# First chunk of a hybrid decoder layer: two column tiles of its projection worked on half of its tokens at a time

## The chip, the core and the metric

The kernel runs on one core of one Trainium2 chip. The metric is the device time in microseconds of one execution. The engines are PE (TensorE: matmuls and transposes), DVE (VectorE), ACT (ScalarE), POOL (GpSimd) and SP (SyncE, which here only issues DMAs). Each engine works through its own queue in order, and waits on semaphores of the others.

## The reference

One layer, 2048 tokens of width 1024. A root-mean-square norm, one projection to 4096 columns that are split in six parts, two token mixers (a state-space branch on `ua`, a pooling branch on `ub`) with gates, an output projection, a residual and a second norm. All in float32.

```python
def _rmsnorm(x, g):
    x32 = x.astype(jnp.float32)
    y = x32 * lax.rsqrt(jnp.mean(x32 * x32, axis=-1, keepdims=True) + EPS)
    return y.astype(x.dtype) * g

h = _rmsnorm(x, norm_g[l])
proj = h @ w_in[l] + b_in[l]
ua, za, ub, zb, ga, gb = jnp.split(proj, SPLITS, axis=-1)
...
merged = (jax.nn.sigmoid(ga) * (ya @ w_branch_a[l])
          + jax.nn.sigmoid(gb) * (yb @ w_branch_b[l]))
x = x + merged @ w_out[l]
return _rmsnorm(x, final_norm_g)
```

## The kernel before

The tokens are worked in four chunks `c` of 512, the columns of the projection in tiles `n` of 128. A chunk is four x tiles of 128 tokens by 1024. Each is normed (sum of squares, reciprocal root, scaling), and turned by PE transposes into `hT[c]`, which has the 1024 channels as eight blocks `k` of 128 partitions, and 512 tokens as columns.

Float32 precision comes from splitting every operand in a high and a low part, both in the format fp32r: `split` (line 94) has ACT write the high part (L96), and then another engine subtract it from the source for the low part (L98 with plain sources on DVE or POOL, L100 with a scale, on DVE). `mm3` (line 103) then issues three matmuls, L104 high by high, L105 high by low part of hT, L106 low part of the weights by high. So L105 needs DVE's low part of hT, and L106 the low part of the weight tile.

`rsqrt` (line 108) has nine tiny DVE instructions, L113 to L122, behind one for the mean (L545). Weight tiles pass through `pump` (line 133): it splits the next loaded weight tile and issues a further load (`load_next`, L163, on SP's queue, two raw buffers). For the input projection the low part of the weights is made on POOL.

`first_block` (line 565) is the special start: four x tiles of chunk 0 are squared on ACT (`mean_square`, L543), one root for all four, then each tile is scaled in two halves of its channels, two tiles on ACT (L574), two on DVE (L576). `transpose_tile` (line 559, L562) turns one block `k` of all four tiles into one PSUM tile of 512 columns and splits it. Blocks are turned two ahead of the eight steps of the first column tile. The second column tile of chunk 0, and all later ones, are `proj_block` (line 593): 24 matmuls with 512 columns in a row. PSUM tiles for transposes (`mstile`) have four buffers, and so have those for the projection (`mmtile`).

The order of the program's work is the order in which the code calls the engines; nothing reorders it. In the loop at line 628 the first chunk's column tile 0 is followed by `pump` (third weight tile, `w_first`), the bias and store of the tile (L637, L638), the norm of chunk 1 (`norm_tiles`), then column tile 1, `pump` for the fourth weight tile, tile 2, four transposed blocks of chunk 1, tile 3 and four more blocks. Loads are issued by SP in this order: four x tiles of chunk 0, weight tiles 0 and 1 (W0, W1 below; W2 and W3 are the third and fourth), four x tiles of chunk 1, W2, chunk 2. Before all this, `WARM` transposes of the identity run on PE (L623).

Of the kernel before, what the change touches and what calls it, by code (L numbers as in the profile page):

```python
# [9 lines left out]
F32 = mybir.dt.float32  # L10
# [3 lines left out]
ALU = mybir.AluOpType  # L14
# [15 lines left out]
WINDOWS = (2, 4, 8, 16)  # L30
EPS = 1e-6
MAGIC = 12582912.0
WARM = 17


@with_exitstack
def hybrid_kernel(ctx: ExitStack, tc: tile.TileContext, x, norm_g, w_in, b_in, log_dt, lam_re, lam_im,
# [31 lines left out]
    def mmtile(name="mm"):  # L69
        return pmm.tile([128, 512], F32, tag="mm", name=name)  # L70

    def mstile(name="ms"):
        return pms.tile([128, 512], F32, tag="ms", name=name)
# [20 lines left out]
    def split(src, hi, lo, scale=None, eng=None):  # L94

        A.activation(hi, src, AF.Copy, scale=1.0 if scale is None else scale)  # L96
        if scale is None:
            (eng or V).tensor_tensor(out=lo, in0=src, in1=hi.bitcast(F32), op=ALU.subtract)  # L98
        else:
            V.scalar_tensor_tensor(out=lo, in0=src, scalar=scale, in1=hi.bitcast(F32),  # L100
                                   op0=ALU.mult, op1=ALU.subtract)
# [28 lines left out]
    def add_job(key, load, target):  # L130
        jobs.append((key, load, target))

    def pump():

        j = state["split"]
        while state["loaded"] < min(j + 2, len(jobs)):
            load_next()
        key, raw, target = jobs[j][0], jobs[j][3], jobs[j][2]
        hi, lo, view = target(key)
        split(view(raw), hi, lo, scale={"ya": 0.125, "yb": 0.5}.get(key[0]), eng=GP if key[0] in ("in", "out", "glu") else V)  # L140
        state["split"] = j + 1
        if state["loaded"] < len(jobs):
            load_next()

# [372 lines left out]

    xts = {}

    def load_x(c):  # L520

        for i in range(4):
            tt = 4 * c + i
            if c in (1, 2):
                xt = xp.tile([128, D], F32, tag="xt", bufs=8, name="xt")
            else:
                xt = d1.tile([128, D], F32, tag="xt", bufs=4, name="xt")
            k0 = (tt % 2) * 128
            SP.dma_start(out=xt, in_=xr[tt // 2, k0:k0 + 128, :])
            xts[tt] = xt  # L530
# [28 lines left out]
    def transpose_tile(c, k):  # L559
        ps = mstile("psT")  # L560
        for i in range(4):
            PE.transpose(ps[:, i * 128:(i + 1) * 128], xts[4 * c + i][:, k * 128:(k + 1) * 128], idn)  # L562
        split(ps, hT[c][:, 0, k, :], hT[c][:, 1, k, :], scale=gcol(k))

    def first_block():

        rstd = mean_square(0)
        pump()

        def scale(h):  # L570
            for i in range(4):
                xt = xts[i][:, h * 512:(h + 1) * 512]
                if i % 2:
                    A.activation(xt, xt, AF.Copy, scale=rstd[:, i:i + 1])  # L574
                else:
                    V.tensor_scalar(out=xt, in0=xt, scalar1=rstd[:, i:i + 1], scalar2=None, op0=ALU.mult)  # L576

        load_x(2)
        scale(0)
        transpose_tile(0, 0)  # L580
        transpose_tile(0, 1)
        scale(1)
        ps = mmtile()
        w = hl[("in", UA)].rearrange("p s (k n) -> p s k n", k=NK)
        for k in range(NK):
            if k + 2 < NK:
                transpose_tile(0, k + 2)
            if k == 3:
                pump()
            mm3(ps, w[:, 0, k, :], w[:, 1, k, :], hT[0][:, 0, k, :], hT[0][:, 1, k, :], k == 0, k == NK - 1)  # L590
        return ps

    def proj_block(n, c):
        ps = mmtile()
# [5 lines left out]
    warm = d1.tile([128, 1], F32, name="warm")  # L600
    GP.memset(warm, 0.0)
    A.activation(warm, warm, AF.Tanh)
    load_x(0)
    rows = d1.tile([48, 128], F32, name="rows")
    A.dma_start(out=rows[0:32, :], in_=b_in[0].rearrange("(n p) -> n p", p=128))
    A.dma_start(out=rows[32:40, :], in_=norm_g[0].rearrange("(n p) -> n p", p=128))
# [14 lines left out]
    psw = mstile("psw")  # L621
    for i in range(WARM):
        PE.transpose(psw[:, (i % 4) * 128:(i % 4 + 1) * 128], idn, idn)  # L623
    load_next()
    load_next()
    load_x(1)
    pv = Later(V)
    for c in range(NCH):
        for n in range(NB):
            ps = proj_block(UA + n, c) if c or n else first_block()  # L630
            if c == 0 and n < 2:
                pump()
            if c == 0 and n == 0:
                small = load_params(par)
                load_x(3)
            o = stg.tile([128, 512], F32, tag="stg", name="uo")
            A.activation(o, ps, AF.Identity, bias=bcol(UA + n))  # L637
            A.dma_start(out=Ud[n][2 * c:2 * c + 2].rearrange("j g c k -> (g c) j k"),  # L638
                         in_=o.rearrange("p (j k) -> p j k", j=2))
            if c + 1 < NCH:  # L640
                if n == 0 and c == 0:
                    norm_tiles(1)
                if n >= 2:
                    for k in range(4 * n - 8, 4 * n - 4):
                        transpose_tile(c + 1, k)
                    if (c, n) == (1, 3):
                        s_x.close()
                        open_hT(3)
                if n == 3 and c + 2 < NCH:
                    norm_tiles(c + 2)  # L650
            if c == NCH - 1 and n < 2:
                pump()
            if (c, n) == (1, 0):
                params(par, pv, *small)
            pv.issue(18)
# [570 lines left out]
```

## Time and profile before

| | |
|---|---|
| median of 3 runs | 1210.48 us (1209.46 to 1212.61) |
| profiled execution | 1210.43 us |
| its span | 1208.6 us |
| PE busy | 1177.1 us, 97% |
| DVE busy | 735.7 us, 61% |
| ACT busy | 395.4 us, 33% |
| POOL busy | 345.6 us, 29% |

The span is the time from the first to the last recorded instruction; the execution has 1.8 us more around it. Busy time of PE overlaps itself, since a matmul starts before the one ahead has ended: for PE the spacing of starts says how long a piece of work takes. A row of the timeline that has "x4" stands for four instructions in a row, and its length is that of all. What stands in brackets is how long the engine was idle, and what ended that.

### The profile page before, as it was taken

The numbers are of one execution on the slowest core, as the hardware profiler recorded it, in microseconds if no ns is written. First come the engines' busy times: TensorE is split into PE (matmuls) and PEld (weight loads), VectorE is DVE, ScalarE is ACT, GpSimd is POOL, SyncE is SP. The second block draws the span as 40 slices with busy tenths as digits, with TensorE's granted clock in tenths as the row PEclk, the third lists the DMA queues.
The fourth block names the chain that finished last, engine by engine and source line by source line (L and its number), as shares of the span: only waits on it lengthen the run. The fifth ranks groups of instructions, "written<-read, shape, count | busy, mean of one in ns | idle before, by whom it ended". The sixth has DMA issues, their size and how long they took to land. (4 is left out here: it accounts for less than half of the span.)

```text
span 1208.6 us, 14777 instructions
## 1 busy us (share of the span) xinstructions
PE 1177.1 (97%) x5413; PEld 974.5 (81%) x5413; DVE 735.7 (61%) x1310; ACT 395.4 (33%) x622; POOL 345.6 (29%) x232
## 2 busy tenths in 40 slices
PE   6999999999999999999999999999999999999996
PEld 5887877888888888888888888887888888888885
DVE  5588299154443667877788773055665855755715
ACT  6543212222222232444324432244333332322302
POOL 3231086012011122432234321224552312313312
PEclk9999999999999999999999999999999999999998
DMA  7412334201111232433333332278766563663603
GB/s 286 151 36 68 86 98 145 82 18 57 50 38 55 95 97 93 126 109 112 97 109 118 98 105 79 75 227 261 248 219 220 179 197 132 186 209 105 192 1 104
DMA packets 149783, 149.94 MB, mean 124 GB/s; under 512 B 23584, under 2 KB 111184, under 8 KB 149712
## 3 DMA queue, kind: packets, MB, share of 16 engines
q1 hardware_dynamic: 127424, 112.28, 30.7%
q10 hardware_dynamic: 22288, 36.73, 8.1%
q8 instruction: 42, 0.69, 0.2%
q14 instruction: 29, 0.24, 0.1%
HBM read 99.43 MB, written 49.55 MB: 123 GB/s over the span
## 5 line engine op out<-in xcount | busy, mean ns | idle before, releaser
L104 PE MATMUL mm<-hT,wt 128*128 128x512 f32 x960 | 376.2, 392 | 0.0
L105 PE MATMUL mm<-hT,wt 128*128 128x512 f32 x960 | 374.8, 390 | 0.5 <-DVE hT L100 0.5
L106 PE MATMUL mm<-hT,wt 128*128 128x512 f32 x960 | 374.2, 390 | 0.0
L105 PEld LDWEIGHTS mm<-hT,wt 128*128 128x128 f32 x960 | 180.6, 188 | 38.4 <-DVE hT L100 1.9
L106 PEld LDWEIGHTS mm<-hT,wt 128*128 128x128 f32 x960 | 180.5, 188 | 37.7
L104 PEld LDWEIGHTS mm<-hT,wt 128*128 128x128 f32 x960 | 180.6, 188 | 36.8
L98 POOL TENSOR_TENSOR wt<-raw,wt 128x1024 fp32r<-128x1024 f32 x30 | 84.9, 2831 | 303.9 <-ACT wt L96 303.9
L1028 ACT ACTIVATE go<-mm,half 128x512 f32<-128x512 f32 x64 | 44.0, 687 | 193.0 <-PE mm L106 192.6
L104 PE MATMUL mm<-yab,wt 128*128 128x512 f32 x256 | 99.8, 390 | 0.7 <-DVE gt L1162 0.7
L105 PE MATMUL mm<-yab,wt 128*128 128x512 f32 x256 | 99.6, 389 | 0.0
L106 PE MATMUL mm<-yab,wt 128*128 128x512 f32 x256 | 99.6, 389 | 0.0
L96 ACT ACTIVATE wt<-raw 128x1024 fp32r<-128x1024 f32 x62 | 65.6, 1058 | 59.9 <-PE mm L106 28.2
L1164 POOL TENSOR_TENSOR m<-gt 128x512 f32<-128x512 f32 x32 | 52.2, 1631 | 96.6 <-DVE gt L1162 76.4
L1122 POOL TENSOR_TENSOR r<-r,gb 128x512 f32<-128x512 f32 (+1 forms) x33 | 41.0, 1258 | 135.1 <-ACT xt L1119 135.1
L98 DVE TENSOR_TENSOR wt<-raw,wt 128x1024 fp32r<-128x1024 f32 x32 | 59.1, 1846 | 19.0 <-ACT wt L96 18.8
L846 ACT ACTIVATE st<-mm,half 128x512 f32<-128x512 f32 x32 | 22.1, 689 | 131.2 <-PE mm L106 72.2
L1162 DVE SCALAR_TENSOR_TENSOR gt<-gt,mm 128x512 f32<-128x512 f32 x64 | 42.3, 680 | 28.6 <-PE mm L106 23.9
L104 PEld LDWEIGHTS mm<-yab,wt 128*128 128x128 f32 x256 | 48.0, 188 | 11.6 <-DVE gt L1162 0.8
L105 PEld LDWEIGHTS mm<-yab,wt 128*128 128x128 f32 x256 | 48.0, 188 | 10.0
L106 PEld LDWEIGHTS mm<-yab,wt 128*128 128x128 f32 x256 | 48.0, 188 | 9.8
L105 PE MATMUL mm<-wo,mt 128*128 128x512 f32 (+1 forms) x136 | 51.2, 377 | 0.0
L106 PE MATMUL mm<-wo,mt 128*128 128x512 f32 (+1 forms) x136 | 51.2, 376 | 0.0
(272 smaller groups left out, 1922.9 us busy)
## 6 DMA issues: line engine op xcount, KB each, us to landing
xt<-in_x SPq DMA_DIRECT2D x32, 512.0 KB, 4.8
raw<-in_w_in SPq DMA_DIRECT2D x32, 512.0 KB, 4.2
Gd<-go ACTq DMA_DIRECT2D x64, 256.0 KB, 2.1
gt<-Gd SPq DMA_DIRECT2D x32, 512.0 KB, 4.7
raw<-in_w_branch_a SPq DMA_DIRECT2D x32, 256.0 KB, 2.9
raw<-in_w_branch_b SPq DMA_DIRECT2D x32, 256.0 KB, 3.3
out<-r ACTq DMA_DIRECT2D x32, 256.0 KB, 2.3
Ud<-uo ACTq DMA_DIRECT2D x16, 256.0 KB, 2.1
```

The source lines that it names most:

```text
L96: A.activation(hi, src, AF.Copy, scale=1.0 if scale is None else scale)
L98: (eng or V).tensor_tensor(out=lo, in0=src, in1=hi.bitcast(F32), op=ALU.subtract)
L104: PE.matmul(ps, lhsT=sh, rhs=mh, start=first, stop=False)
L105: PE.matmul(ps, lhsT=sh, rhs=ml, start=False, stop=False)
L106: PE.matmul(ps, lhsT=sl, rhs=mh, start=False, stop=last)
L846: A.activation(t, ps, AF.Tanh, bias=hcol(n), scale=0.5)
L1028: A.activation(o, ps, AF.Tanh, bias=hcol(n), scale=0.5)
L1122: GP.tensor_tensor(out=r, in0=r, in1=gb[:, cs], op=ALU.mult)
L1162: V.scalar_tensor_tensor(out=gt[:, b], in0=gt[:, b], scalar=1.0, in1=pss[b], op0=ALU.add, op1=ALU.mult)
L1164: GP.tensor_tensor(out=m, in0=gt[:, 0], in1=gt[:, 1], op=ALU.add)
```

## The change

`first_block` becomes `first_blocks`, which does column tiles 0 and 1 of chunk 0 on two halves `h` of the tokens (two x tiles, 256 columns each). For half 0: tile 0 is squared on ACT, tile 1 on DVE, one root, scaling, and per block `k` a transposed PSUM tile of 256 columns (`turn`), split as before; then eight steps of column tile 0 with 256 columns (`step`). Half 1 is squared (one tile on ACT, one on DVE) and its root taken in the middle of these steps, at `k == 3`; its scaling comes behind them. Then the eight steps of column tile 1 on half 0 go in turn with the eight `turn`s of half 1, and at last both column tiles are done on half 1.

The first weight tile's low part is now made on DVE, in two halves (`rest`), instead of on POOL. Weight tiles 0 and 1 are loaded between and behind the x tiles of chunk 0, W2 behind the x tiles of chunks 1 and 2. `WARM` is 11 instead of 17.

```diff
--- before.py
+++ after.py
@@ -30,7 +30,7 @@
 WINDOWS = (2, 4, 8, 16)
 EPS = 1e-6
 MAGIC = 12582912.0
-WARM = 17
+WARM = 11
 
 
 @with_exitstack
@@ -130,15 +130,23 @@
     def add_job(key, load, target):
         jobs.append((key, load, target))
 
-    def pump():
+    def pump(later=None):
 
         j = state["split"]
         while state["loaded"] < min(j + 2, len(jobs)):
             load_next()
         key, raw, target = jobs[j][0], jobs[j][3], jobs[j][2]
         hi, lo, view = target(key)
-        split(view(raw), hi, lo, scale={"ya": 0.125, "yb": 0.5}.get(key[0]), eng=GP if key[0] in ("in", "out", "glu") else V)
+        if later:
+            A.activation(hi, raw, AF.Copy)
+        else:
+            split(view(raw), hi, lo, scale={"ya": 0.125, "yb": 0.5}.get(key[0]), eng=GP if key[0] in ("in", "out", "glu") else V)
         state["split"] = j + 1
+        if later:
+            def rest(h):
+                cs = slice(512 * h, 512 * h + 512)
+                later.tensor_tensor(out=lo[:, cs], in0=raw[:, cs], in1=hi[:, cs].bitcast(F32), op=ALU.subtract)
+            return rest
         if state["loaded"] < len(jobs):
             load_next()
 
@@ -517,9 +525,9 @@
 
     xts = {}
 
-    def load_x(c):
-
-        for i in range(4):
+    def load_x(c, tiles=range(4)):
+
+        for i in tiles:
             tt = 4 * c + i
             if c in (1, 2):
                 xt = xp.tile([128, D], F32, tag="xt", bufs=8, name="xt")
@@ -562,33 +570,73 @@
             PE.transpose(ps[:, i * 128:(i + 1) * 128], xts[4 * c + i][:, k * 128:(k + 1) * 128], idn)
         split(ps, hT[c][:, 0, k, :], hT[c][:, 1, k, :], scale=gcol(k))
 
-    def first_block():
-
-        rstd = mean_square(0)
-        pump()
-
-        def scale(h):
-            for i in range(4):
-                xt = xts[i][:, h * 512:(h + 1) * 512]
-                if i % 2:
+    def first_blocks():
+
+        ss = [d1.tile([128, 2], F32, name=f"ss{h}") for h in range(2)]
+
+        def square(h, i):
+            xt, at = xts[2 * h + i], ss[h][:, i:i + 1]
+            land = hT[1][:, i, 0:2, :].rearrange("p k n -> p (k n)")
+            if i == 0:
+                A.activation(land, xt, AF.Square, accum_out=at)
+            else:
+                V.scalar_tensor_tensor(out=land, in0=xt, scalar=1.0, in1=xt, op0=ALU.mult, op1=ALU.mult, accum_out=at)
+
+        def root(h):
+            v = d1.tile([128, 2], F32, name=f"v{h}")
+            V.tensor_scalar(out=v, in0=ss[h], scalar1=1.0 / D, scalar2=EPS, op0=ALU.mult, op1=ALU.add)
+            return rsqrt(d1, v, 2)
+
+        def scale(h, rstd, part):
+            for i in range(2):
+                xt = xts[2 * h + i][:, part * 512:(part + 1) * 512]
+                if i:
                     A.activation(xt, xt, AF.Copy, scale=rstd[:, i:i + 1])
                 else:
                     V.tensor_scalar(out=xt, in0=xt, scalar1=rstd[:, i:i + 1], scalar2=None, op0=ALU.mult)
 
+        def turn(h, k):
+            ps = mstile("psT")[:, 0:256]
+            for i in range(2):
+                PE.transpose(ps[:, i * 128:(i + 1) * 128], xts[2 * h + i][:, k * 128:(k + 1) * 128], idn)
+            r = slice(256 * h, 256 * h + 256)
+            split(ps, hT[0][:, 0, k, r], hT[0][:, 1, k, r], scale=gcol(k))
+
+        def step(n, h, k):
+            w = hl[("in", UA + n)].rearrange("p s (k n) -> p s k n", k=NK)
+            r = slice(256 * h, 256 * h + 256)
+            mm3(pss[n][:, r], w[:, 0, k, :], w[:, 1, k, :], hT[0][:, 0, k, r], hT[0][:, 1, k, r], k == 0, k == NK - 1)
+
         load_x(2)
-        scale(0)
-        transpose_tile(0, 0)
-        transpose_tile(0, 1)
-        scale(1)
-        ps = mmtile()
-        w = hl[("in", UA)].rearrange("p s (k n) -> p s k n", k=NK)
+        square(0, 0)
+        square(0, 1)
+        rstd = root(0)
+        rest = pump(V)
+        square(1, 0)
+        scale(0, rstd, 0)
+        turn(0, 0)
+        rest(0)
+        turn(0, 1)
+        scale(0, rstd, 1)
+        rest(1)
+        pss = [mmtile(), mmtile()]
         for k in range(NK):
             if k + 2 < NK:
-                transpose_tile(0, k + 2)
+                turn(0, k + 2)
             if k == 3:
                 pump()
-            mm3(ps, w[:, 0, k, :], w[:, 1, k, :], hT[0][:, 0, k, :], hT[0][:, 1, k, :], k == 0, k == NK - 1)
-        return ps
+                square(1, 1)
+                rstd = root(1)
+            step(0, 0, k)
+        scale(1, rstd, 0)
+        scale(1, rstd, 1)
+        for k in range(NK):
+            step(1, 0, k)
+            turn(1, k)
+        for n in range(2):
+            for k in range(NK):
+                step(n, 1, k)
+        return pss
 
     def proj_block(n, c):
         ps = mmtile()
@@ -600,7 +648,10 @@
     warm = d1.tile([128, 1], F32, name="warm")
     GP.memset(warm, 0.0)
     A.activation(warm, warm, AF.Tanh)
-    load_x(0)
+    load_x(0, (0, 1))
+    load_next()
+    load_x(0, (2, 3))
+    load_next()
     rows = d1.tile([48, 128], F32, name="rows")
     A.dma_start(out=rows[0:32, :], in_=b_in[0].rearrange("(n p) -> n p", p=128))
     A.dma_start(out=rows[32:40, :], in_=norm_g[0].rearrange("(n p) -> n p", p=128))
@@ -621,13 +672,13 @@
     psw = mstile("psw")
     for i in range(WARM):
         PE.transpose(psw[:, (i % 4) * 128:(i % 4 + 1) * 128], idn, idn)
-    load_next()
-    load_next()
     load_x(1)
     pv = Later(V)
     for c in range(NCH):
         for n in range(NB):
-            ps = proj_block(UA + n, c) if c or n else first_block()
+            if c == n == 0:
+                pss = first_blocks()
+            ps = proj_block(UA + n, c) if c or n > 1 else pss[n]
             if c == 0 and n < 2:
                 pump()
             if c == 0 and n == 0:
```

On DVE, the start of chunk 0. `hT_174` is hT of chunk 0, `hT_178` that of chunk 1, whose space takes the squares; `rsy`, `rsq`, `rsh` are the root's tiles. Before, behind the one root:

```order
L576 TENSOR_SCALAR xt<-xt,rsy 128x512 x2
L100 SCALAR_TENSOR_TENSOR hT_174<-psT,cols,hT_174 128x512 x2
L576 TENSOR_SCALAR xt<-xt,rsy 128x512 x2
L100 SCALAR_TENSOR_TENSOR hT_174<-psT,cols,hT_174 128x512 x6
L538 SCALAR_TENSOR_TENSOR hT_178,ss<-xt 128x1024 x2
L545 TENSOR_SCALAR v<-ss 128x4
```

Now, behind the root of half 0 (the rows from L583 on are the square of x tile 3 and the first two of the ten instructions of the second root):

```order
L596 TENSOR_SCALAR xt<-xt,rsy 128x512
L100 SCALAR_TENSOR_TENSOR hT_174<-psT,cols,hT_174 128x256
L148 TENSOR_TENSOR wt<-raw,wt 128x512
L100 SCALAR_TENSOR_TENSOR hT_174<-psT,cols,hT_174 128x256
L596 TENSOR_SCALAR xt<-xt,rsy 128x512
L148 TENSOR_TENSOR wt<-raw,wt 128x512
L100 SCALAR_TENSOR_TENSOR hT_174<-psT,cols,hT_174 128x256 x4
L583 SCALAR_TENSOR_TENSOR hT_178,ss_269<-xt 128x1024
L587 TENSOR_SCALAR v_352<-ss_269 128x2
L113 TENSOR_SCALAR rsy<-v_352 128x2
```

and behind the last instruction of the second root:

```order
L122 SCALAR_TENSOR_TENSOR rsy<-rsq,rsy 128x2
L100 SCALAR_TENSOR_TENSOR hT_174<-psT,cols,hT_174 128x256 x2
L596 TENSOR_SCALAR xt<-xt,rsy 128x512 x2
L100 SCALAR_TENSOR_TENSOR hT_174<-psT,cols,hT_174 128x256 x8
L546 SCALAR_TENSOR_TENSOR hT_178,ss<-xt 128x1024 x2
```

The square of an x tile and a second root now stand between the low parts of blocks 0 to 5 and those of blocks 6 and 7, and the low part of the first weight tile stands between those of the first blocks.

On ACT, the same place. Before (L543 squares, L96 with `wt<-raw` the high part of a weight tile, L574 the scaling):

```order
L543 ACTIVATE hT_174,ss<-xt 128x1024 x4
L96 ACTIVATE wt<-raw 128x1024
L574 ACTIVATE xt<-xt,rsy 128x512 x2
L96 ACTIVATE hT_174<-psT,cols 128x512 x2
L574 ACTIVATE xt<-xt,rsy 128x512 x2
L96 ACTIVATE hT_174<-psT,cols 128x512 x4
L96 ACTIVATE wt<-raw 128x1024
L96 ACTIVATE hT_174<-psT,cols 128x512 x2
L96 ACTIVATE w_first_193<-raw 128x1024
```

Now (L581 squares, L141 the high part of the first weight tile, L594 the scaling):

```order
L581 ACTIVATE hT_178,ss_268<-xt 128x1024
L141 ACTIVATE wt<-raw 128x1024
L581 ACTIVATE hT_178,ss_269<-xt 128x1024
L594 ACTIVATE xt<-xt,rsy 128x512
L96 ACTIVATE hT_174<-psT,cols 128x256 x2
L594 ACTIVATE xt<-xt,rsy 128x512
L96 ACTIVATE hT_174<-psT,cols 128x256 x4
L96 ACTIVATE wt<-raw 128x1024
L96 ACTIVATE hT_174<-psT,cols 128x256 x2
L594 ACTIVATE xt<-xt,rsy 128x512 x2
L96 ACTIVATE hT_174<-psT,cols 128x256 x8
```

The high part of the second weight tile still stands ahead of those of the blocks 6 and 7, behind block 5; two of the squares have gone to DVE.

On SP, the loads of the start. Before:

```order
L529 DMA xt<-in_x 128x1024 x4
L163 DMA raw<-in_w_in 128x8x128 x2
L529 DMA xt<-in_x 128x1024 x4
L163 DMA raw<-in_w_in 128x8x128
L529 DMA xt<-in_x 128x1024 x4
L163 DMA raw<-in_w_in 128x8x128 x2
```

Now:

```order
L537 DMA xt<-in_x 128x1024 x2
L171 DMA raw<-in_w_in 128x8x128
L537 DMA xt<-in_x 128x1024 x2
L171 DMA raw<-in_w_in 128x8x128
L537 DMA xt<-in_x 128x1024 x8
L171 DMA raw<-in_w_in 128x8x128 x3
```

The first weight tile comes third instead of fifth, and the third and fourth come behind eight x tiles instead of four.

## Rows read from the trace of the kernel before

**Rows 1.** The page, part 1: busy time, share of the span, instructions.

```profile
PE 1177.1 (97%) x5413; PEld 974.5 (81%) x5413; DVE 735.7 (61%) x1310; ACT 395.4 (33%) x622; POOL 345.6 (29%) x232
```

**Rows 2.** Timeline to 14.3 us: start, length (us), engine, line, operation [idle before].

```profile
7.60 0.20 DVE L613 TENSOR_SCALAR half<-psr 128x48 f32<-128x48 f32 x1
...
9.65 0.17 DVE L545 TENSOR_SCALAR v<-ss 128x4 f32<-128x4 f32 x1 [1.85 <-ACT hT L543]
...
10.15 1.06 ACT L96 ACTIVATE wt<-raw 128x1024 fp32r<-128x1024 f32 x1 [0.54 <-DMA raw<-in_w_in]
...
11.29 2.34 POOL L98 TENSOR_TENSOR wt<-raw,wt 128x1024 fp32r<-128x1024 f32 x1 [8.85 <-ACT wt L96]
...
11.45 2.21 DVE L122 SCALAR_TENSOR_TENSOR rsy<-rsq,rsy 128x4 f32<-128x4 f32 x1
...
13.69 1.34 ACT L574 ACTIVATE xt<-xt,rsy 128x512 f32<-128x512 f32 x2 [2.48 <-DVE rsy L122]
...
13.69 0.88 DVE L576 TENSOR_SCALAR xt<-xt,rsy 128x512 f32<-128x512 f32 x2
...
14.23 3.03 PE L562 MATMUL psT<-idn,xt 128*128 128x128 f32 x12 [2.97 <-DVE xt L576]
```

**Rows 3.** Timeline of PE, first block, 17 to 27 us.

```profile
17.48 0.63 PE L105 MATMUL mm<-hT,wt 128*128 128x512 f32 x1
...
17.91 0.63 PE L106 MATMUL mm<-hT,wt 128*128 128x512 f32 x1
...
19.62 0.54 PE L105 MATMUL mm<-hT,wt 128*128 128x512 f32 x1
...
26.36 0.39 PE L104 MATMUL mm<-hT,wt 128*128 128x512 f32 x1
```

**Rows 4.** Timeline of POOL and DVE, 23 to 31 us.

```profile
23.72 2.40 POOL L98 TENSOR_TENSOR wt<-raw,wt 128x1024 fp32r<-128x1024 f32 x1 [10.08 <-ACT wt L96]
...
24.25 1.50 DVE L100 SCALAR_TENSOR_TENSOR hT<-psT,cols,hT 128x512 fp32r<-128x512 f32 x2 [0.77 <-ACT hT L96]
...
26.08 3.39 POOL L98 TENSOR_TENSOR w_first<-raw,w_first 128x1024 fp32r<-128x1024 f32 x1
...
27.24 3.31 DVE L538 SCALAR_TENSOR_TENSOR hT<-xt 128x1024 fp32r<-128x1024 f32 x1
...
30.66 0.17 DVE L545 TENSOR_SCALAR v<-ss 128x4 f32<-128x4 f32 x1
```

**Rows 5.** Timeline of PE, last projection, first and last of 48 matmuls.

```profile
1192.25 0.28 PE L104 MATMUL mm<-wo,mt 128*128 128x256 f32 x1
...
1197.89 0.28 PE L106 MATMUL mm<-wo,mt 128*128 128x256 f32 x1
```

**Rows 6.** Groups by form: count, busy us, mean ns, idle before.

```profile
L703 ACT ACTIVATE xs<-psx 64x256 f32<-64x256 f32 x64 | 24.3, 379 | 10.4 <-PE psx L106 9.3 <-ACT go L1028 0.4
...
L100 DVE SCALAR_TENSOR_TENSOR hT<-psT,cols,hT 128x512 fp32r<-128x512 f32 x32 | 22.3, 745 | 14.4 <-ACT hT L96 14.3
...
L738 DVE TENSOR_TENSOR tmp<-tab,UB 128x512 f32<-128x512 f32 x16 | 10.4, 689 | 0.3
...
L738 DVE TENSOR_TENSOR tmp<-tab,UB 128x256 f32<-128x256 f32 x16 | 6.1, 422 | 0.3
```

**Rows 7.** Timeline of ACT, POOL and PE, 26 to 40 us.

```profile
26.56 0.69 ACT L637 ACTIVATE uo<-mm,cols 128x512 f32<-128x512 f32 x1 [0.66 <-PE mm L106]
...
29.89 0.18 ACT L543 ACTIVATION_READ_ACCUMULATOR hT<-xt 128x1 f32 x1
...
35.93 2.38 POOL L98 TENSOR_TENSOR w_first<-raw,w_first 128x1024 fp32r<-128x1024 f32 x1 [6.47 <-ACT w_first L96]
...
37.43 1.91 PE L562 MATMUL psT<-idn,xt 128*128 128x128 f32 x16
...
39.65 0.39 PE L106 MATMUL mm<-hT,w_first 128*128 128x512 f32 x1
```

**Rows 8.** Stretch 14 to 24 us: busy of five engines, PEclk, DMA share, GB/s.

```profile
14.00:24.00 10.00, 9.77 (x48) 8.29 (x48) 5.86 (x10) 7.57 (x12) 0.28 (x1) 1.00 0.88 341
```

## The prediction

> **What bounds the kernel now.** I read the page's busy shares first: PE, the matrix engine, is busy 97% of the span [rows 1], so what the start loses or wins on PE is carried to the end, if nothing later takes it back. Next the timeline of the first 40 us. Until 26.36 us PE is led by others; from there the matmuls follow one another without a gap. The first real transposes start at 14.23 us, after 2.97 us in which PE waited for the scaled x tiles [rows 2]. Behind that wait stands a chain on DVE: sum of squares, ten tiny instructions for the reciprocal root, then the scaling. The tenth tiny instruction, L122, is the one to look at: it takes 2.21 us where its neighbours take 0.17, and it ends 0.03 us after POOL's 2.34 us subtraction for the first weight tile [rows 2]. So POOL's instruction holds DVE up, and this costs the old start 2.05 us. The same is seen at 27.24 us: the square L538 takes 3.31 us, and POOL's instruction beside it ends at 29.47, 1.08 us before it [rows 4]. An instruction on DVE that reads PSUM is not held: two of them take 1.50 us in the middle of POOL's 2.40 us [rows 4]. That pair of facts decides my forecast.
>
> **PE's own work.** Matmuls of 512 columns at full speed follow each other every 0.231 us: 48 of them lie between 26.36 and 37.43 us [rows 3, 7]. Those of 256 columns follow every 0.120 us: 47 steps from 1192.25 to 1197.89 us [rows 5]. Sixteen transposes take 1.91 us, 0.12 each [rows 7]. In the first block two matmuls start 0.43 us apart, at 17.48 and 17.91, and last 0.63 us; at 19.62 one lasts 0.54, at 26.36 0.39 [rows 3]: PE ran there at half speed until about 19.7. The granted clock of 14 to 24 us reads 1.00, which is the 2.4 GHz level [rows 8], although in its first half the spacing is that of the 1.2 GHz level; I go by the spacing.
>
> **The change, along its critical chain** (us from the start of the span, all times estimates from the rows named).
>
> 1. DVE is free at 7.80, after the two copies of the bias columns [rows 2]. It now squares x tile 1 itself: 1.08 us by rows 4. The square ends at 8.9 and the root (1.80 us from its first to its last start, and 0.17) at 10.9 [rows 2]. W0 landed at about 10.1 as fifth in SP's queue [rows 2] and now comes third, so ACT can split it in the time of the root; its low part moves from POOL to DVE, so L122 isn't held. The scaled tiles are there at 11.6 (0.67 us on ACT) [rows 2], where they were at 14.23 before: 2.6 us earlier.
> 2. Two transposes at half speed (0.45 us until they can be read, an estimate from the 0.43 spacing) and a 256-wide high part on ACT, 0.4 us by the nearest row, 0.38 for 256 columns [rows 6]: 12.5 us. WARM falls from 17 to 11 transposes; these lie in PE's wait and cost nothing.
> 3. DVE now has six low parts from PSUM before tile 3 is squared. A 512-wide one takes 0.75 us, and 256 columns less are worth 0.27 us (0.69 against 0.42 for a like pair), so I take 0.4 at a run [rows 6]. With two halves of W0's low part at 0.65 and one scaling at 0.44 [rows 2, 6] this is 4.1 us, up to 16.6. PE is later: at half speed a step k is two transposes and three matmuls, about 1.05 us, and the transposes of k = 5 stand behind step 2. That gives their high part at 17.1 and their low part at 17.5.
> 4. Square of x tile 3, 1.08 us: 18.6.
> 5. ACT puts W1's high part (1.06 us, as W0's [rows 2]) behind the high part of k = 5, so POOL asks for its 2.34 us at 18.2, waits for the square, and runs from 18.6 to 21.0. In this time DVE would start the second root. All of that root reads SBUF, as L122 does, and is held. I take the whole 2.3 us, as rows 2 and 4 show it twice; below, the case that it costs nothing.
> 6. Second root 2.0 us: 23.0. Only then come the low parts of k = 6 and 7 (0.8 us), which stand behind it in DVE's queue. PE is through with the first half of column tile 0 at 24.2. It has stood idle since step 5, about 18.7, for some 4.7 us.
> 7. What is left for PE: 72 matmuls of 256 columns (8.64 us) and 16 transposes (1.9 us), 10.5 us. The third column tile starts at 34.7. Before, it started 24 matmuls ahead of 37.43 [rows 7], at 31.9. **Term: +2.8 us.** In it 96 short matmuls against 48 long ones account for 0.4 us.
> 8. The fourth weight tile. Its split on POOL ended 11.75 us after column tile 0 went to ACT at 26.56 [rows 7], of which 0.6 were DVE's held square (ACT's squares end at 30.07, the next step starts at 30.66) [rows 4, 7]: 11.15 without it. Now the two tiles end 2.9 us apart instead of 5.5, so column tile 0 goes out at 32.0 and the split ends at 43.2. PE wants it at 39.65 - 31.9 = 7.75 us behind the third tile's start [rows 7], at 42.45. **Term: +0.7 us**, a new wait of L106 on POOL.
> 9. PE's speed. Before, it ran at half speed from the first transposes to about 19.7, that is 5.5 us [rows 2, 3]. Whether the 4.7 us gap of step 6 throws it back, no row of before shows. If it doesn't, this costs 0; if it does and the ramp is as long as the old one, half of 5.5 us, 2.7. I take 0.8: counted from row 17.48 the old ramp was 2.2 us, which would cost 1.1, and a fall is somewhat less likely than none. **Term: +0.8 us.**
>
> The Trainium skill, "TensorE: Matmul & The Clock Gate", section "What's actually happening", says that the throttled clock is the default and returns after an idle stretch. By the row alone the term is between 0 and 2.7; by this rule it would be the 2.7.
>
> Sum: 2.8 + 0.7 + 0.8 = +4.3 us. The profiled execution took 1210.43 us, the median of the runs is 1210.48, so they can be taken as one: **1214.7 us**.
>
> Edits that cost nothing: the loads of x chunks 1 and 2 now stand ahead of W2 in SP's queue, but W2 is wanted only at 34.7. POOL loses one split that nobody waits for any more.
>
> **The rivals.**
>
> - *PE falls back to half speed in the gap.* For it: 4.7 us of idle and then a cold start, as at 14.23. Against: before shows no such fall. It has the full 2.7 instead of 0.8: 1210.4 + 6.2 = 1216.6 us. This is the rule of the page named above; no row here shows it. Chance 0.18.
> - *POOL's split of W1 hides behind the low parts, and the change is not slower.* They read PSUM and aren't held [rows 4]. It decides whether ACT has W1's high part ready by about 16.3, that is 2.3 us before DVE reaches the second root; ACT's order speaks against it, since W1 stands behind k = 5. Then step 5 costs nothing: 2.8 - 2.3 + 0.7 and a shorter gap with 0.3 for the speed, +1.5, 1211.9 us. Chance 0.22.
> - *The whole start runs at DVE's own pace*: no wait on PE in step 3 (-0.9), no POOL in step 5, the fourth tile in time: 2.8 - 2.3 - 0.9 = -0.4, 1210.0 us. Even so it isn't faster by a measurable amount. Chance 0.05, with whatever could be faster still.
>
> **How the numbers follow.** About 0.3%, 3.6 us, is what a measurement of this kernel can tell from no change. The forecast case has 0.52, its own range is +2.8 (term 9 nil, step 3 without PE's wait) to +5.5, and about six tenths of it lie above 3.6. A cause not seen here, slower still, has 0.03. Slower: 0.31 + 0.18 + 0.03 = 0.52. Within 0.3%: 0.21 + 0.22 and a little of the last rival, 0.44. Faster: 0.04. The range reaches from the second rival with 1 us to spare, 1210.9, to the first one, 1216.9.
>
> **What would show it.** First transposes at 11.4 to 12 us. L122 of the first root at 0.17 us, and in the second root one DVE instruction of over 2 us that ends with POOL's W1 split. Low parts of k = 6 and 7 at about 23 us, and a PE wait of over 4 us in front of them. The third column tile at 34 to 35.5 us, where 31.9 stood. L106 of the fourth waiting on POOL for under 1 us. After that everything shifted by the same amount, with the same work. I am wrong if the second root runs free of POOL, or if PE's wait in front of k = 6 is under 2 us; and wrong upwards if the matmuls from 24 to 30 us follow at 0.21 instead of 0.12.

## The result, and the profile after

The changed kernel takes **1218.66 us** (median of 5 runs, 1217.17 to 1219.53); the kernel before, run beside it, 1211.34 us (5 runs, 1209.46 to 1212.61). The ratio is 1.0063, with a 95% interval of 1.0052 to 1.0075: slower, by 7.3 us between the medians (6.3 to 9.1 us by the interval). The forecast, +4.3 us, has the right sign and most of the mechanism, but is too small, and its range ended 1.8 us too low. The profiled execution took 1217.17 us with a span of 1215.3, 6.7 us more than the span before.

Page, part 1, of the changed kernel (answers to [rows 1]):

```profile
PE 1179.0 (97%) x5455; PEld 977.8 (80%) x5455; DVE 743.9 (61%) x1334; ACT 395.0 (32%) x626; POOL 342.6 (28%) x231
```

PE's share is the same. Its busy time grew by 1.9 us, so most of the loss must be waiting. The waits of PE say where (line, what it waited for, us in total, times, longest):

```profile
PE mm L105 <- DVE hT L100: 4.8, 3, 4.4
...
PE psT L601 <- DVE xt L596: 1.6, 1, 1.6
...
PE mm L106 <- POOL w_first L98: 0.6, 1, 0.6
```

The wait for scaled x tiles fell to 1.6 us (2.97 in [rows 2]); a wait of 4.4 for a low part on DVE and one of 0.6 for POOL are new. Timeline of DVE and POOL, from the bias columns to the second half's scaling (start, length, operation, idle before):

```profile
8.12 0.20 DVE L664 TENSOR_SCALAR half<-psr 128x48 f32<-128x48 f32 x1
8.23 1.22 DVE L583 SCALAR_TENSOR_TENSOR hT<-xt 128x1024 fp32r<-128x1024 f32 x1
...
9.57 0.17 DVE L587 TENSOR_SCALAR v<-ss 128x2 f32<-128x2 f32 x1
...
11.35 0.16 DVE L122 SCALAR_TENSOR_TENSOR rsy<-rsq,rsy 128x2 f32<-128x2 f32 x1
...
18.17 0.48 DVE L100 SCALAR_TENSOR_TENSOR hT<-psT,cols,hT 128x256 fp32r<-128x256 f32 x1 [0.58 <-ACT hT L96]
18.57 1.22 DVE L583 SCALAR_TENSOR_TENSOR hT<-xt 128x1024 fp32r<-128x1024 f32 x1
...
19.17 2.81 POOL L98 TENSOR_TENSOR wt<-raw,wt 128x1024 fp32r<-128x1024 f32 x1 [16.73 <-ACT wt L96]
...
19.83 2.18 DVE L587 TENSOR_SCALAR v<-ss 128x2 f32<-128x2 f32 x1
...
23.63 0.16 DVE L122 SCALAR_TENSOR_TENSOR rsy<-rsq,rsy 128x2 f32<-128x2 f32 x1
23.71 0.87 DVE L100 SCALAR_TENSOR_TENSOR hT<-psT,cols,hT 128x256 fp32r<-128x256 f32 x2
```

L122 of the first root takes 0.16 us, where it took 2.21 [rows 2]. The instruction that is held now is L587, the first of the second root: 0.17 us the first time, 2.18 the second, and it ends at 22.01, 0.03 us after POOL's subtraction (19.17 + 2.81 = 21.98). Behind it in DVE's queue stand the rest of the root and then the low parts of k = 6 and 7, at 23.71. PE waits for these (timeline of PE, same columns; answers to [rows 3]):

```profile
17.84 0.28 PE L106 MATMUL mm<-hT,wt 128*128 128x256 f32 x1
...
18.30 0.28 PE L105 MATMUL mm<-hT,wt 128*128 128x256 f32 x1
18.41 0.28 PE L106 MATMUL mm<-hT,wt 128*128 128x256 f32 x1
...
24.24 0.38 PE L105 MATMUL mm<-hT,wt 128*128 128x256 f32 x1 [4.35 <-DVE hT L100]
...
25.23 0.41 PE L104 MATMUL mm<-hT,wt 128*128 128x256 f32 x1
25.44 0.41 PE L105 MATMUL mm<-hT,wt 128*128 128x256 f32 x1
...
28.49 0.28 PE L106 MATMUL mm<-hT,wt 128*128 128x256 f32 x1
28.61 0.38 PE L601 MATMUL psT<-idn,xt 128*128 128x128 f32 x2
...
36.88 0.40 PE L104 MATMUL mm<-hT,w_first 128*128 128x512 f32 x1
...
45.45 0.50 PE L106 MATMUL mm<-hT,w_first 128*128 128x512 f32 x1 [0.58 <-POOL w_first L98]
```

Matmuls of 256 columns follow at 0.12 us before the gap and after 28.4, but 0.21 apart in between. Here the granted clock says it too (stretches from 24.24 on: busy of five engines, PEclk, DMA share, GB/s):

```profile
24.24:24.70 0.46, 0.46 (x3) 0.46 (x4) 0.46 (x2) 0.46 (x2) 0.00 (x0) 0.93 1.14 347
24.70:25.90 1.20, 1.20 (x8) 1.20 (x7) 0.67 (x2) 0.46 (x1) 0.00 (x0) 0.50 0.51 152
25.90:28.00 2.10, 2.10 (x11) 2.10 (x11) 0.48 (x1) 0.87 (x2) 0.00 (x0) 0.50 0.00 0
28.00:36.88 8.88, 8.88 (x76) 8.88 (x76) 7.84 (x11) 6.02 (x12) 2.89 (x1) 1.00 0.09 32
```

0.50 is the 1.2 GHz level. PE had stood idle for 4.35 us, worked again for 0.4 us at 2.4 GHz, and then ran some 3.3 us at half speed, which costs half of that, some 1.6 us.

The third column tile starts at 36.88. In the trace of the kernel before:

```profile
31.83 0.40 PE L104 MATMUL mm<-hT,w_first 128*128 128x512 f32 x1
```

That is +5.05. The fourth weight tile adds 0.85 (16 transposes to the next 16: 42.49 to 50.69 now, 37.43 to 44.78 before). From there the two traces run 5.9 to 6.0 us apart (first GLU output at 424.6 against 418.6) up to some 800 us; the last 0.7 us of the span's difference come behind that.

### The profile page after: what moved, and what is told of

Its sections match the earlier page's. It is cut to its first block, busy times and chain, and to the rows that moved or that the text cites. A ratio compares the mean times of both kernels' runs of the same rounds, so it can differ in the third digit from the quotient of the medians.

```text
span 1215.3 us, 14890 instructions
## 1 busy us (share of the span) xinstructions
PE 1179.0 (97%) x5455; PEld 977.8 (80%) x5455; DVE 743.9 (61%) x1334; ACT 395.0 (32%) x626; POOL 342.6 (28%) x231
## 5 line engine op out<-in xcount | busy, mean ns | idle before, releaser
L105 PE MATMUL mm<-hT,wt 128*128 128x512 f32 (+1 forms) x976 | 378.4, 388 | 4.8 <-DVE hT L100 4.8
L104 PE MATMUL mm<-hT,wt 128*128 128x512 f32 (+1 forms) x976 | 380.5, 390 | 0.2 <-ACT hT L96 0.2
L106 PE MATMUL mm<-hT,wt 128*128 128x512 f32 (+1 forms) x976 | 377.8, 387 | 0.0
L105 PEld LDWEIGHTS mm<-hT,wt 128*128 128x128 f32 x976 | 184.5, 189 | 42.5 <-DVE hT L100 6.1
L106 PEld LDWEIGHTS mm<-hT,wt 128*128 128x128 f32 x976 | 184.3, 189 | 37.3 <-DVE wt L148 0.3
L104 PEld LDWEIGHTS mm<-hT,wt 128*128 128x128 f32 x976 | 184.4, 189 | 36.9 <-ACT hT L96 0.4
L106 PE MATMUL mm<-yab,wt 128*128 128x512 f32 x256 | 99.6, 389 | 0.0
L96 ACT ACTIVATE wt<-raw 128x1024 fp32r<-128x1024 f32 x61 | 64.5, 1057 | 57.4 <-PE mm L106 32.6
L106 PEld LDWEIGHTS mm<-yab,wt 128*128 128x128 f32 x256 | 48.0, 188 | 10.1
L106 PE MATMUL mm<-wo,mt 128*128 128x512 f32 (+1 forms) x136 | 51.2, 376 | 0.0
```

The costliest lines, as they stand in the source:

```text
L104: PE.matmul(ps, lhsT=sh, rhs=mh, start=first, stop=False)
L105: PE.matmul(ps, lhsT=sh, rhs=ml, start=False, stop=False)
L106: PE.matmul(ps, lhsT=sl, rhs=mh, start=False, stop=last)
```

## The experiments

Times of one execution's start are sharper than totals, so the experiments are read at a landmark: the first matmul of the third column tile. For the kernels with halves one more correction helps. There DVE's first work waits for a DMA, the rows of biases, which PE first used between 7.38 and 7.73 us; the fifth column counts from this use (psr). The two kernels with whole blocks (before and e3) need none: their root waits for ACT's fourth square, and starts at 9.65 with psr at 7.13 and at 9.58 with psr at 7.33. They are compared by the fourth column.

Each landmark is that of one execution, and differences under some 0.6 us say little: the changed kernel, e2 and e4 have the same program up to the low part of k = 5, yet DVE starts it 10.52, 10.25 and 9.90 us behind psr.

| kernel | psr | PE resumes at k = 6 | third tile | third tile from psr | ratio to before |
|---|---|---|---|---|---|
| before | 7.13 | – | 31.83 | – | 1 |
| changed | 7.65 | 24.24 | 36.88 | 29.23 | 1.0063 |
| e1_w1_early | 7.53 | 21.55 | 34.21 | 26.68 | 1.0040 |
| e2_busy_gap | 7.38 | 23.72 | 34.82 | 27.44 | 1.0040 |
| e3_w0_on_dve | 7.33 | – | 29.29 | – | 0.9994 |
| e4_root_later | 7.70 | – | 33.74 | 26.04 | 1.0046 |
| e5_halves_mended | 7.55 | – | 32.48 | 24.93 | 1.0042 |
| e6_warm17 | 7.43 | 23.38 | 35.98 | 28.55 | 1.0044 (one run) |
| e7_early_and_busy | 7.73 | 21.98 | 33.07 | 25.34 | 1.0027 |

The ratios are to runs of the kernel before on the same chip, whose median was 1209.97 us beside e1 to e4 (17 runs) and 1210.35 beside e5 to e7 (12 runs). The theory: POOL's split of W1 holds the second root, PE's gap follows, and the clock falls in the gap. Rivals: the order in DVE's queue alone makes the gap; or the halves are dear in themselves.

**W1's split earlier** (`e1_w1_early`), on the changed kernel:

```diff
-            if k == 3:
+            if k == 0:
                 pump()
+            if k == 3:
                 square(1, 1)
                 rstd = root(1)
```

> The changed kernel, with the split of the second weight tile (W1) asked for at k = 0 instead of k = 3, so that POOL's subtraction lies beside DVE's low parts from PSUM and is over before the second root. Theory (POOL holds the second root up for 2.2 us, and the long gap this makes in PE's work throws PE back to half speed): the first instruction of the second root takes 0.2 instead of 2.2 us, PE's wait in front of the low part of k = 6 falls from 4.35 to 2.2 us or less, the third column tile starts at 33.5 to 34.8 us instead of 37.0; 2.2 us faster than the changed kernel if the half speed remains, 3.4 if it goes; still 3 to 4 us slower than the kernel before. Rival (the chain of square and root in DVE's queue is what costs, POOL is beside it): less than 0.7 us from the changed kernel.

1214.67 us (5 runs, 1214.29 to 1215.60), ratio 1.0040 (1.0027 to 1.0054). Timelines of POOL, DVE and PE, then the clock:

```profile
15.63 2.40 POOL L98 TENSOR_TENSOR wt<-raw,wt 128x1024 fp32r<-128x1024 f32 x1 [13.19 <-ACT wt L96]
...
17.43 0.48 DVE L100 SCALAR_TENSOR_TENSOR hT<-psT,cols,hT 128x256 fp32r<-128x256 f32 x1 [0.22 <-ACT hT L96]
...
19.15 0.17 DVE L587 TENSOR_SCALAR v<-ss 128x2 f32<-128x2 f32 x1
...
21.55 0.39 PE L105 MATMUL mm<-hT,wt 128*128 128x256 f32 x1 [2.96 <-DVE hT L100]
```

```profile
21.55:22.60 1.05, 1.05 (x8) 1.05 (x9) 1.05 (x3) 0.92 (x2) 0.00 (x0) 0.98 1.15 346
22.60:25.90 3.30, 3.30 (x18) 3.30 (x17) 1.04 (x3) 1.37 (x3) 0.00 (x0) 0.50 0.43 130
```

POOL works beside low parts that read PSUM, and L587 is back at 0.17 us: the hold is shown, and worth 2.0 us by itself. From psr the third tile comes 2.55 us earlier; what is over 2.0 is a square that started 0.6 us sooner from psr. That much can be chance. In the trace's list of the granted clock the first stretch at full speed, which ends the slow start, begins at 15.74 us here and at 17.81 in the changed kernel, but at 15.80 in e4 too, where W1's split isn't moved. The order of DVE's queue remains, and with it a gap of 2.96 us (2.2 or less was expected), behind which the clock falls just the same.

**Work for PE in the gap** (`e2_busy_gap`), on the changed kernel; the transposes go to a PSUM tile that nothing reads:

```diff
+            if k == 6:
+                psd = mmtile("psd")
+                for i in range(36):
+                    PE.transpose(psd[:, (i % 4) * 128:(i % 4 + 1) * 128], idn, idn)
             step(0, 0, k)
```

> The changed kernel with 36 transposes of the identity on PE in the gap in front of step 6, whose result is not used. Theory (the gap throws PE back to half speed): matmuls after the gap follow at 0.12 us from the first one on, the third column tile starts at 35.7 instead of 37.0, 1.2 us faster than the changed kernel. Rival (the 0.21 us spacing behind the gap is a wait for ACT or DVE, or the speed is set otherwise): the spacing stays at 0.21 for some 3 us and the time the same within 0.4 us.

1214.53 us (5 runs, 1213.91 to 1215.84), ratio 1.0040 (1.0026 to 1.0053). PE and DVE, then the clock:

```profile
18.51 4.09 PE L633 MATMUL psd<-idn 128*128 128x128 f32 x36
...
19.29 2.21 DVE L587 TENSOR_SCALAR v<-ss 128x2 f32<-128x2 f32 x1
...
23.72 0.39 PE L105 MATMUL mm<-hT,wt 128*128 128x256 f32 x1 [0.99 <-DVE hT L100]
```

```profile
25.00:27.00 2.00, 2.00 (x19) 2.00 (x18) 1.07 (x3) 1.46 (x4) 0.00 (x0) 1.00 0.04 8
```

DVE is held as in the changed kernel, PE waits as long for its data, but it was busy for 4.09 us of it, and the clock stays at 1.00. From psr PE resumes 0.25 us earlier (16.34 against 16.59) and reaches the third tile 1.79 earlier. The difference, 1.5 us, is what the half speed costs (1.2 was expected).

**Both** (`e7_early_and_busy`): e1's edit with e2's, 24 transposes instead of 36.

> The changed kernel with both remedies of the two earlier runs: the second weight tile split at k = 0, and 24 transposes of the identity in the gap in front of step 6. Theory (POOL's hold and the fall to half speed are two costs that add): no half-speed matmul behind the gap, third column tile at 32.6 to 33.1 us, that is 1.1 to 1.6 us ahead of the run with the early split alone. Rival (they are one cost, the half speed follows from POOL's hold and goes with it, or the filling does all): no earlier than 33.8.

1213.29 us (8 runs, 1211.92 to 1215.70), ratio 1.0027 (1.0017 to 1.0037).

```profile
21.98:24.00 2.02, 2.02 (x17) 2.02 (x18) 1.13 (x4) 1.40 (x3) 0.00 (x0) 1.00 1.06 317
```

Against e1 it resumes 0.23 us later from psr and is at the third tile 1.34 earlier: 1.6 us for the half speed again. From psr the third tile is 3.89 us ahead of the changed kernel's, and the rows add up to that: 2.0 for the hold, 0.3 for a square that starts 10.60 instead of 10.92 us behind psr, 1.6 for the half speed. So hold and half speed are two costs that add. (The gains of e1 and e2 by themselves, 2.55 and 1.79, come to more, 4.34, since both have a sooner square in them.) At 33.07 the third tile is still 1.24 us later than before's; that part wasn't taken apart. The profiled execution, 1215.70 us, is the longest of the eight.

**The second root behind all low parts** (`e4_root_later`), with the later steps put in a matching order:

```diff
             if k == 3:
                 pump()
-                square(1, 1)
-                rstd = root(1)
             step(0, 0, k)
+        square(1, 1)
+        rstd = root(1)
         scale(1, rstd, 0)
...
         for k in range(NK):
             step(1, 0, k)
-            turn(1, k)
-        for n in range(2):
-            for k in range(NK):
-                step(n, 1, k)
+        turn(1, 0)
+        turn(1, 1)
+        for k in range(NK):
+            if k + 2 < NK:
+                turn(1, k + 2)
+            step(0, 1, k)
+        for k in range(NK):
+            step(1, 1, k)
```

> The changed kernel in another order: square and root of the second half stand behind the low parts of all eight blocks, and the eight steps of column tile 1 on the first half come before the transposes of the second half. POOL's split of W1 is left where it is. Theory (the wait is DVE's queue: the low parts of k = 6 and 7 stand behind square, POOL and root): no PE wait over 0.5 us in front of k = 6; PE is through with both column tiles on the first half at about 23.7 us, and waits there for the scaling of the second half until about 25.3; third column tile at 34 to 34.7 us, 2.3 to 3 us faster than the changed kernel. Rival (the whole work of the second half is what is late, wherever it stands): the same wait of over 4 us shows up in front of the transposes, and less than 1 us is won.

1215.04 us (6 runs, 1214.49 to 1217.16), ratio 1.0046 (1.0032 to 1.0061). Timeline of DVE, then waits of PE:

```profile
19.70 2.35 DVE L583 SCALAR_TENSOR_TENSOR hT<-xt 128x1024 fp32r<-128x1024 f32 x1
```

```profile
PE mm L106 <- POOL w_first L98: 1.0, 1, 1.0
PE psT L601 <- PE mm L106: 0.7, 1, 0.7
PE mm L104 <- ACT hT L96: 0.5, 2, 0.3
```

POOL still holds DVE, now its square (2.35 us, where 1.22 is usual), but PE has the first half's low parts by then. No wait between the first step and the third tile is over 0.7 us, the clock doesn't fall, and from psr the third tile comes 3.19 us earlier. So the rival about the queue's order is right in part: hold and order make the gap together. With the order changed no long gap is left, though POOL holds DVE; with the hold gone, in e1, 2.96 of the 4.35 us remain. The run has two edits, the root behind the low parts and column tile 1 ahead of the transposes, which weren't tried apart. The gain shrinks on the way, since the fourth weight tile is now waited for by 1.0 us.

**Halves with every wait seen so far taken away** (`e5_halves_mended`): e4, with W1 split at k = 0, and W3 split directly behind W2:

```diff
-            if c == 0 and n < 2:
+            if c == 0 and n == 0:
                 pump()
-            if c == 0 and n == 0:
+                pump()
```

> The changed kernel with the second weight tile split at k = 0, square and root of the second half behind the low parts of all blocks and column tile 1 on the first half ahead of the second half's transposes (the two earlier edits together), and the fourth weight tile split right behind the third, so that PE doesn't wait for it. Theory (three separate costs: POOL's hold, the queue order with the half speed it brings, the late fourth tile): third column tile at 32 to 33 us, no wait of PE on POOL for the fourth tile, 4 to 5 us faster than the changed kernel and 0.5 to 2 us slower than the kernel before, since the halves start 2 us sooner but have 96 matmuls in place of 48, and the second half's tiles wait for a root of their own. Rival (something else in the halves costs): still over 2.5 us slower than the kernel before. Other rival: the halves mended beat the kernel before by over 1 us.

1215.77 us (5 runs, 1213.80 to 1216.78), ratio 1.0042 (1.0028 to 1.0055). Up to the third tile it goes as expected, 32.48. Then POOL and DVE:

```profile
29.72 6.23 POOL L98 TENSOR_TENSOR w_first<-raw,w_first 128x1024 fp32r<-128x1024 f32 x2 [11.70 <-ACT w_first L96]
...
30.39 3.31 DVE L546 SCALAR_TENSOR_TENSOR hT<-xt 128x1024 fp32r<-128x1024 f32 x1
...
34.02 1.95 DVE L553 TENSOR_SCALAR v<-ss 128x4 f32<-128x4 f32 x1 [0.32 <-ACT hT L551]
```

W3 is in time, but the two splits in a row hold the square and the root of chunk 1, whose scaled tiles PE then waits for twice, 0.5 us each. The total gains 2.5 us on the changed kernel (ratios of 1.0042 and 1.0063, times 1210 us), less than was expected. Against the kernel before it is 5.4 us slower (1215.77 and 1210.35) where 0.5 to 2 were expected, so the rival that something else costs came true. Little of it lies in the first block: the third tile is 0.65 us later than before's, the trace is 2.3 us behind from 107 us on, and the rest comes behind 800 us, where it wasn't followed.

**The one part alone** (`e3_w0_on_dve`): the kernel before, whole blocks of 512 tokens, with only the low part of W0 moved from POOL to DVE, in halves behind the scalings, and the load of W2 that `pump` issued put behind it (the diff leaves out `pump(later)`, which is that of the change):

```diff
-        pump()
+        rest = pump(V)
...
         transpose_tile(0, 0)
+        rest(0)
         transpose_tile(0, 1)
         scale(1)
+        rest(1)
+        load_next()
```

> The kernel before with one part of the change alone: the low part of the first weight tile (W0) is made on DVE in two halves behind the low parts of the first blocks, not on POOL beside the root. Theory (POOL held the first root up for 2.05 us, and that was worth something): the last instruction of the root takes 0.2 instead of 2.2 us, the first transposes start at 12.2 instead of 14.2; of the 2 us some is lost again as PE is at half speed for longer and the low parts stand behind the halves, so 1 to 2 us faster than the kernel before. Rival (the ramp to full speed bounds the start, not the root): the third column tile still starts at 31.5 or later, within 0.5 us of the kernel before.

1209.35 us (11 runs, 1207.54 to 1212.19), ratio 0.9994 (0.9984 to 1.0004). Timeline of ACT, DVE and PE:

```profile
8.40 1.06 ACT L551 ACTIVATE hT<-xt 128x1024 fp32r<-128x1024 f32 x1
...
9.58 0.17 DVE L553 TENSOR_SCALAR v<-ss 128x4 f32<-128x4 f32 x1 [1.58 <-ACT hT L551]
...
11.38 0.16 DVE L122 SCALAR_TENSOR_TENSOR rsy<-rsq,rsy 128x4 f32<-128x4 f32 x1
...
12.12 3.03 PE L570 MATMUL psT<-idn,xt 128*128 128x128 f32 x12 [0.65 <-DVE xt L584]
```

This is the sharpest of the seven. With all four x tiles in the sum of squares, all on ACT, the root starts at 9.58 and the first transposes at 12.12. In the changed kernel, with two tiles, they start at 9.57 and 12.10: its square on DVE stands behind the bias columns and ends no sooner than ACT's fourth. In the seven kernels with halves the first transposes start between 11.83 and 12.17. So working on half of the tokens brings the start forward by 0.3 us at most; the move of W0's low part away from POOL does nearly all. This holds for the queues as they stand. In the changed kernel x tile 1 landed at 5.91 us, but its square is behind the copies of the bias columns in DVE's queue and started at 8.23. Halves with that square ahead of the copies weren't run, and could start earlier.

At the third tile e3 is 2.5 us ahead of before, and still at 97 us (a column tile leaves PE's PSUM at 94.66, before at 97.22); it is 1.8 us ahead at the next one (105.73 and 107.49) and 1.0 at the last projection. The step from 2.5 to 1.8 is the clock again. In front of the transposes of chunk 3, PE waits for DVE (e3's row and clock, then those of the kernel before):

```profile
96.17 3.09 PE L570 MATMUL psT<-idn,xt 128*128 128x128 f32 x16 [1.55 <-DVE hT L100]
97.75:101.10 3.35, 3.35 (x13) 2.83 (x12) 2.97 (x18) 1.84 (x3) 0.00 (x0) 0.50 0.00 0
```

```profile
98.73 2.63 PE L562 MATMUL psT<-idn,xt 128*128 128x128 f32 x16 [1.55 <-DVE hT L100]
100.30:103.70 3.40, 3.40 (x19) 2.73 (x18) 3.02 (x18) 1.79 (x3) 0.00 (x0) 1.00 0.00 0
```

The same wait was followed by a fall in the executions of e3, e6 and e7, and by none in the six others (the wait is 1.2 to 1.6 us in all nine). In the total no difference of e3 from before can be told, where 1 to 2 us were expected. It has the lowest time of the versions, and is 0.7% under the changed kernel (0.9994 against 1.0063).

**17 warm-up transposes again** (`e6_warm17`, one run): `WARM = 17` in the changed kernel.

> The changed kernel with 17 transposes of the identity ahead of the start, as before, instead of 11. Theory (they lie in PE's wait for the first scaled tiles and cost nothing): first transposes at 12.1 us as now, the same PE wait in front of the low part of k = 6; PE may come to full speed a little sooner, but DVE leads there, so the third column tile starts within 0.5 us of 36.9. Rival (the shorter run-up is why the start is at half speed for so long, and this costs): third column tile 1 us or more earlier.

One run of 1215.63 us. PE is at full spacing by 14.94 instead of 17.84:

```profile
14.82 0.28 PE L105 MATMUL mm<-hT,wt 128*128 128x256 f32 x1
14.94 0.28 PE L106 MATMUL mm<-hT,wt 128*128 128x256 f32 x1
...
23.38 0.38 PE L105 MATMUL mm<-hT,wt 128*128 128x256 f32 x1 [4.35 <-DVE hT L100]
```

Nearly 3 us of faster PE become 0.7 at the third tile (from psr), because PE waits 4.35 us for DVE all the same and the clock falls behind it again. At the first GLU output nothing is left (424.5, 424.6 in the changed kernel): behind the wait in front of chunk 3's transposes (1.58 us, the changed kernel's is 1.57) the clock fell in this execution, and not in the changed kernel's.

Whether the 0.7 us belong to WARM isn't shown. The slow clock of the start ended at 13.41 us here, but with 17 transposes also at 15.82 (e3) and 19.92 (before), and with 11 anywhere from 15.74 to 17.81. And e4, with 11, started the low part of k = 5 9.90 us behind psr, e6 9.88.

## Why the prediction was right or wrong

Its mechanism stands: the first root is freed, POOL's split of W1 holds one instruction of the second root, k = 6 and 7 stand behind that root, PE waits over 4 us, the clock falls, and the fourth weight tile is late. The sizes, by its steps:

- **Steps 1 and 2** (scaled tiles at 11.6, first high part done at 12.5): scaling ended at 12.04 for DVE's tile, and the high part at 13.3. The bias rows were there 0.5 us later than in [rows 2]. All seven kernels with the new order of loads have them at 7.38 to 7.73, the two with the old order at 7.13 and 7.33; whether the order does it or chance, no run shows. The square took 1.22 us, not the 1.08 read from rows 4.
- **Steps 3 to 6**: low part of k = 5 done at 18.57 (17.5 was said), square to 19.8 (18.6), hold of 2.18 us (2.3), root's end at 23.79 (23.0). Step 6 named PE's gap as 4.7 us: 4.35. Each point is 0.8 to 1.2 us late, 0.5 of it the bias rows'; the held instruction, the order and the gap are as written. The rival in which POOL's split hides fell, and by the condition it named: in e1, where W1's high part is ready early, the split does hide.
- **Step 7**, the rest of PE's work: 72 short matmuls and 16 transposes take 10.35 us at full speed (8 groups of 0.575, 48 matmuls of 0.12), 10.5 said. The term +2.8 came out near +3.5 without the clock: 5.05 less 1.5.
- **Step 8**, the fourth weight tile: +0.85, said +0.7, with the wait of L106 on POOL that it named.
- **Step 9 is the step that failed, by its size.** It took 0.8 us for a fall of the clock and gave the full fall a chance of 0.18, since no row of before showed one, and the rival says that before shows none. That is a misreading. The trace of before has one (PE's row, then the stretch behind it):

```profile
835.25 0.49 PE L104 MATMUL mm<-yhl,wg 128*128 128x512 f32 x1 [2.59 <-ACT yhl L96]
835.70:839.10 3.40, 3.17 (x8) 2.48 (x8) 3.36 (x6) 2.60 (x5) 0.00 (x0) 0.50 0.98 257
```

  After 2.59 us of waiting PE ran 3.4 us at the 1.2 GHz level, which costs half of that, 1.7 us. At the start the clock falls in every kernel here whose PE stood idle for 3 to 4.35 us in front of k = 6 (the changed one, e1, e6), and not when transposes fill the gap (e2, e7). It costs 1.5 to 1.6 us. By the page of the Trainium skill that the prediction weighed ("TensorE: Matmul & The Clock Gate", section "What's actually happening") the slow clock returns after idling; the runs agree that it does so after the long gaps. The price is less than the 2.7 us that the prediction worked out from the old ramp, because the slow stretch after the gap lasted 3.3 us and not 5.5.
- **WARM at 11 "costs nothing"** is neither shown nor refuted: e6 is 0.7 us ahead at the third tile, about what executions with 11 differ by.

Against a predicted sum of 4.3 us the trace shows 5.05 + 0.85 = 5.9 by 51 us. Of the miss of 1.6, 0.7 are step 9's, 0.15 step 8's, the rest the later chain of steps 1 to 7. All this together would still lie inside the stated range, whose upper end is 6.4 us above the kernel before.

What took the median out of the range is a term that the prediction put at nothing: "After that everything shifted by the same amount". The interval of the ratio, 6.3 to 9.1 us, lies wholly above 5.9. The profiled execution has 0.7 us of it, behind some 800 us. The cause stays open. The four other executions of the changed kernel, 0.8 to 2.4 us longer than the profiled one, have a mean granted clock of 0.992 where it has 0.995. That is what further falls of the clock would give, but no trace of them was kept. Besides, the kernel before took 0.9 us more in the five runs beside the change than in the three that the forecast starts from.

One slip changes nothing: by its own terms the forecast's own range begins at 4.3 - 0.8 - 0.9 = +2.6, not +2.8.

What the prediction didn't see is e3's lesson: it credited the earlier start to the whole change and never asked what four tiles would do without POOL's hold. Its own rows had the answer: ACT's four squares end at 9.6 us, 0.7 us after the 8.9 that step 1 gave to the half, and in the runs even that was gone, as the half's square on DVE came late. With both alike in W0's split, e5's third tile starts at 32.48 and e3's at 29.29. So whole blocks beat these mended halves by 3.2 us at this place. In part this can be read from the traces: the slow clock of the start lasts until 17.30 in e5 and 15.82 in e3, half of which is 0.7 us; between 22.80 and 24.56 no matmul of a column tile starts in e5, since the second half is turned only then; 0.4 us are the short matmuls of step 7. The rest wasn't taken apart.

## What to carry to other kernels

Before splitting a unit to start earlier, take its blocker away in the unsplit version and look whether the start moves; here that one edit gave nearly all of the 2 us, and the split, in the order in which it was queued, cost more than it won. When work is put into an in-order queue, list what stands behind it and who waits: the ten tiny instructions of a root cost 2 us of DVE, another engine's hold doubled that, and a gap in PE then costs once more through its clock. Price a gap on TensorE as its length, plus half of the slow stretch where one follows, and look through the whole trace of the kernel before for such a stretch: here it had one, some 800 us later than the place that was changed.

## What the runs showed of the hardware

- The clock didn't fall at once after the gap. PE resumed at 2.4 GHz for 0.4 us (changed kernel, after 4.35 us idle) or 1.0 us (e1, after 2.96), then ran some 3.3 us at 1.2 GHz in both. Transposes of the identity into a tile that nobody reads kept it at 2.4 GHz (e2, e7).
- Whether the clock falls behind a shorter wait isn't settled by the wait: the one of 1.2 to 1.6 us in front of chunk 3's transposes was followed by a fall in three of nine executions, and each time 0.8 to 0.9 us were lost there.
- The 1.00 that [rows 8] shows for the cold start is not a measured level. The trace's list of the granted clock has its first entry at 19.92 us in the kernel before and at 17.81 in the changed one, and these are the moments at which the spacing of the matmuls changes; time ahead of it is shown as 1.00. There the spacing is the reading to go by, as the prediction did.
- An instruction of DVE on 128 x 2 numbers from SBUF takes 2.18 us instead of 0.17 beside a subtraction on POOL. Low parts that read PSUM are not held: in e1 they run beside POOL's split at their usual 0.48 us. The Trainium skill, "SBUF — State Buffer", section "Who interferes with whom", describes such a lock between DVE and POOL; the runs agree.
